# The copies of rotated q and k on GpSimd's DMA queue alone, in a two-layer hybrid trunk

## The chip, the cores and the metric

One core of a Trainium2 chip. Its engines are PE (TensorE, matmuls), DVE (VectorE), ACT (ScalarE), POOL (GpSimd) and SP (SyncE, which computes nothing and issues transfers). The metric is the device time of one execution in microseconds, as the median of the runs.

## The reference

Two layers over 256 positions of width 1024. Each layer normalises x, projects it by one wide matrix and feeds three mixers, whose outputs are gated, summed, projected and added to x; a squared-ReLU MLP follows. The part that matters here is the attention mixer: 24 heads of width 64 in three groups of eight, with rotary q and k. Rotation pairs the first and second half of a head:

```python
t1, t2 = jnp.split(tf, 2, axis=-1)
return jnp.concatenate([t1 * cos - t2 * sin, t2 * cos + t1 * sin], axis=-1)
...
for g, (window, dilation) in enumerate(DILATED_GROUPS):
    o, lse = dilated_group_attention(qf[:, :, g], kf[:, :, g], vf[:, :, g], window, dilation)
...
o = jnp.sum(wts * o, axis=0).reshape(B, S, ATTN_OUT_WIDTH)
```

The other two mixers are a gated linear recurrence (conv of 4 taps, scan) and a convolution of 31 taps with a layer norm.

## The kernel before

All weights stream through the core as chunks of 1 MB (128 partitions x 2048 floats), 92 in each layer. `weights` (L508) loads a chunk into one of two buffers `raw` through SP's queue, then ACT casts it to the high part `whi` and DVE subtracts that to give the low part `wlo`; a matmul is then done in three products (high by high, high by low, low by high). A `raw` buffer is free again when DVE has made both halves of `wlo`.

Inside a layer the chunks come in the order of the list `ORDER` (L38): v, the recurrence's inputs, the convolution's inputs, then blocks of q and k mixed with gates (`ga`, `gb`, `gc`) and outputs (`oa`, `ob`, `oc`) of the mixers. After that come the output projection, and the MLP's `up` and `dn`.

`rope` (L932) handles one block of q or k: four heads of one group. The matmul leaves the two halves of the heads apart: the first halves of the four heads in column block 0, the second halves in block 1, 32 partitions to a head. DVE makes `r1` from PSUM in three instructions (two products and a sum). For the scores each head needs its 64 rows together, so eight DMA copies of 32 partitions x 256 floats (32 KB) put `r1` into buffers `qk`, one for each head pair `hp` and group `g`. For each of the four heads, the first half goes through POOL's queue and the second through SP's queue (L951). There are twelve blocks in a layer, so 192 copies in all, 96 on each queue. A head pair's scores need six blocks' worth: 24 copies, twelve on each queue.

`scores` (L958) does 12 matmuls for a head pair and a half of the positions into the one PSUM buffer `sc`; DVE then adds the mask and takes the maximum (`sm`, `mx`, L972), ACT the exponential, and PE transposes the result (`tp`).

The order of the instructions on every engine is written out ahead by a planner (`Sched.run`, L252). It simulates the engines with a price for each operation, always takes the ready one with the longest way to the end, and emits the engines' orders. A DMA has two prices: what it occupies its issuing engine (`DMA_ISSUE`, L103: 600 ns on SP and ACT, 1040 ns on POOL) and, on one simulated transfer device, its bytes at 360 per ns with 500 ns ahead of them and 900 ns behind. `WHERE` (L44) names main matmuls before which the eight score groups must have been placed. On the chip each engine works through its list in order and waits for what is not there yet; what stands behind a waiting instruction in its list waits too. POOL's list also holds small memsets (`xp`, `upad`), the loads of the recurrence's gate weights (`lwr`) and gains, and a few tiny arithmetic operations of the norms.

Of the kernel before, what the change touches and what calls it, by code (L numbers as in the profile page):

```python
# [14 lines left out]
T = 256  # L15
# [84 lines left out]
           ("DVE", "PE"): 256, ("PE", "PE"): 2, ("ACT", "ACT"): 143, ("DVE", "DVE"): 127}  # L100
DMA_RATE = 0.36
MARGIN = 15000
DMA_ISSUE, DMA_START, DMA_DONE = {"SP": 600, "POOL": 1040, "ACT": 600}, 500, 900  # L103
LINE = 128
PSUM_TAGS = ("mm", "tp", "sc")
UNPADDED = PSUM_TAGS + ("st",)
# [270 lines left out]
def trunk_kernel(ctx: ExitStack, tc: tile.TileContext, x_d, pos_d, w_d, lruw_d, par_d, gain_d, const_d, id_d, out_d):  # L377
    nc = tc.nc
# [9 lines left out]
    def slot(name, dt=F32, shape=(P, 2, T)):  # L388
        return S.buf(sp, shape, dt, "s2", name, NSLOT)

    def mm_ps(name, shape=(P, 2, T), ring=True):
        return S.buf(pp, shape, F32, "mm", name, 4, ring)
# [13 lines left out]
    def views(*xs):  # L406
        return [x for x in xs if isinstance(x, View)]
# [19 lines left out]
    def tt(out, a, b, op):  # L427
        return S.op("DVE", 1.042 * out.n + 68,
                    lambda: nc.vector.tensor_tensor(out=out.ap(), in0=a.ap(), in1=b.ap(), op=op), [a, b], [out])  # L429
# [18 lines left out]
    def dma(eng, out, in_, nbytes):  # L448
        def fn():
            o = out.ap() if isinstance(out, View) else out  # L450
            i = in_.ap() if isinstance(in_, View) else in_
            eng.dma_start(out=o, in_=i)

        e = {id(nc.gpsimd): "POOL", id(nc.scalar): "ACT"}.get(id(eng), "SP")
        o = S.op(e, DMA_ISSUE[e], fn, views(in_), views(out))
        o.dma = nbytes / DMA_RATE / 1e3
        return o
# [50 lines left out]
    def weights(l, name, spread=False):  # L508
        c = CIDX[name]
        assert c == used[l], (name, c, used[l])  # L510
        used[l] += 1
        nm = f"{name}_{l}"
        raw = S.buf(wp, (P, CHUNK), F32, "raw", f"raw_{nm}", NRAW)
        if l or c:
            o = dma(nc.sync, raw.all(), w_d[l * NCH + c], CHUNK * P * 4)
            if l == 0 and c in late:
                S.follow(o, late[c])
        else:
            for s in range(2):
                o = dma(nc.sync, raw[:, s * HALF:(s + 1) * HALF], w_d[0][:, s * HALF:(s + 1) * HALF], HALF * P * 4)  # L520
                if ORDER[0][0] == "v":
                    S.follow(o, x1_load)
        if spread:
            hs, ls = [], []
            for q in range(4):
                hs.append(slot(f"whi_{nm}{q}", F32R, (P, 512)))
                ls.append(slot(f"wlo_{nm}{q}", F32R, (P, 512)))
                for o in split(hs[q].all(), ls[q].all(), raw[:, q * 512:(q + 1) * 512]):
                    o.prep = True
            return [(Quarters(hs[2 * s:2 * s + 2]), Quarters(ls[2 * s:2 * s + 2])) for s in range(2)]  # L530
        offs = (3 * LINE // 8, LINE // 8) if KIND[name] != "as" else (3 * LINE // 8,) * 2 if name[:2] in ("v1", "v2") else (0, 0)
        hi = Shifted(S.buf(wp, (P, CHUNK + LINE // 2), F32R, "whi", f"whi_{nm}", NHI), offs[0])
        lo = Shifted(S.buf(wp, (P, CHUNK + LINE // 2), F32R, "wlo", f"wlo_{nm}", NHI), offs[1])
        n = HALF if l == 0 and c < 2 else PREP
        for b in range(0, CHUNK, n):
            for o in split(hi[:, b:b + n], lo[:, b:b + n], raw[:, b:b + n]):
                o.prep = True
        return [(Part(hi, s * HALF), Part(lo, s * HALF)) for s in range(2)]
# [204 lines left out]
    for l in range(L):  # L743
# [12 lines left out]
        def gemm(name, w, ps, rhs):  # L756
            n0 = len(S.ops)
            ws_mm(ps, w, rhs)
            starts[name] = S.ops[n0]
# [172 lines left out]
        def rope(nm, g, j):  # L932
            w = weights(l, f"{nm}{g}{j}")
            ps = mm_ps(f"{nm}{g}{j}_{l}")
            gemm(f"{nm}{g}{j}", w, ps, hr)
            t1 = slot(f"r1{nm}{g}{j}_{l}")
            t2 = slot(f"r2{nm}{g}{j}_{l}")
            tt(t1.all(), ps.all(), cosT.all().map(lambda a: a[:, None, :].to_broadcast([P, 2, T])), OP.mult)
            tt(t2.all(), ps.all().map(lambda a: a[:, ::-1, :]), sins.all(), OP.mult)
            tt(t1.all(), t1.all(), t2.all(), OP.add)  # L940
            qi = 0 if nm == "q" else 1
            for hh in range(4):
                hp = 2 * j + hh // 2
                if (hp, g) not in qk:
                    qk[hp, g] = slot(f"qk{hp}{g}_{l}")
                for ab in range(2):
                    p0 = (hh % 2) * 64 + ab * 32
                    d = qk[hp, g]
                    dv = View(d, ((p0, p0 + 32), (qi, qi + 1), (0, T)), T,
                              lambda t, p0=p0: t[p0:p0 + 32, qi, :])  # L950
                    dma(nc.sync if ab else nc.gpsimd, dv, t1[hh * 32:(hh + 1) * 32, ab, :], 32 * T * 4)  # L951

        PTt, pvps, oh, ol = {}, {}, {}, {}
        sm = {}
# [158 lines left out]
        for name in ORDER:  # L1113
            kind, a = name[:2], name[2:]
            if kind in ("oa", "oc", "ob") and kind not in seen:
                {"oa": attention, "oc": layer_norm, "ob": lru_scan}[kind]()
                seen.add(kind)
            if name[0] == "v":
                vproj(int(name[1]), name == ORDER[0])
            elif name[0] in "qk":  # L1120
                rope(name[0], int(name[1]), int(name[2]))
            elif kind in ("ga", "gb", "gc"):
                ths[kind, int(a)] = gate(kind, int(a))
            else:
                {"gl": lambda: glu(int(name[3])), "lx": lambda: lx(int(a)), "lg": lambda: lg(int(a)),
                 "lw": lambda: lru_gates(int(a)), "ob": lambda: lru_out(int(a)), "oa": lambda: attn_out(int(a)),
                 "oc": lambda: conv_out(int(a))}[kind]()
# [219 lines left out]
```

## Time and profile before

| | us |
|---|---|
| median of 3 runs | 1116.06 (1115.8 to 1116.9) |
| the profiled execution | 1113.95 |
| its span, first to last instruction | 1112.2 |
| PE busy | 1095.9 (99%) |
| DVE busy | 902.4 (81%) |
| ACT busy | 727.7 (65%) |
| POOL busy | 70.1 (6%) |

The granted clock of TensorE was 0.999 of full speed. SP's queue carried 200.05 MB, POOL's 8.40 MB. The copies from `r1q` and `r1k` landed 4.4 and 4.6 us after their issue on SP, 3.7 and 4.0 us on POOL (medians). Engine names in rows: PEld is the loading of weights into PE; a q behind an engine (SPq) is its sequencer. Where many instructions follow each other with no idle time, a row merges them and gives their count.

### The profile page before, as it was taken

Reading aid. Unit: us, or ns where it says so; the run is one execution under the profiler, and the core shown is the slowest. Engines: PE = TensorE matmul, PEld = TensorE weight load, DVE = VectorE, ACT = ScalarE, POOL = GpSimd, SP = SyncE. Lnnn points to the kernel's source line nnn. Section 1 sums busy time; section 2 is a strip of 40 time slices with the busy share of each in tenths; the row PEclk is TensorE's granted clock in tenths of the full one; section 3 lists DMA queues with packets and bytes.
Section 4 is the critical chain, followed back from the end, with each engine's and each line's share of the span. In section 5 each row is a group of like instructions: output and inputs, shape, how many; then the busy total and the mean of one; then the engine's idle time right before and its main releaser. Section 6 shows DMA issues by size and latency. Waiting matters only on the chain.

```text
span 1112.2 us, 20605 instructions
## 1 busy us (share of the span) xinstructions
PE 1095.9 (99%) x8258; PEld 1023.9 (92%) x8258; DVE 902.4 (81%) x1380; ACT 727.7 (65%) x1186; POOL 70.1 (6%) x156
## 2 busy tenths in 40 slices
PE   7999999999999999999999999999999999999997
PEld 6999999998899899989889999999988998998996
DVE  6999999999969865555679999999996889655554
ACT  5879948787775454444569896569676746444443
POOL 1000022111000110000000000221200001000000
PEclk9999999999999999999999999999999999999999
DMA  8664466554436565555555553764633364555551
GB/s 294 247 208 152 152 226 236 184 193 149 142 121 245 195 211 197 194 194 189 189 200 215 181 182 116 255 222 171 216 123 143 146 248 161 214 190 189 194 190 71
DMA packets 37650, 209.77 MB, mean 189 GB/s; under 512 B 6449, under 2 KB 9777, under 8 KB 14130
## 3 DMA queue, kind: packets, MB, share of 16 engines
q1 hardware_dynamic: 32976, 200.05, 50.9%
q0 software_dynamic: 4576, 8.40, 2.3%
q8 instruction: 65, 1.06, 0.4%
q14 instruction: 31, 0.25, 0.1%
q10 hardware_dynamic: 2, 0.00, 0.0%
HBM read 201.08 MB, written 1.05 MB: 182 GB/s over the span
## 4 chain that ended last, share of the span: by engine, by line
PE 82%; DVE 10%; ACT 4%; DMA 2%; issue 1%; SPq 0%; DVEq 0%; ACTq 0%
PE dn L476 15%; PE up L476 14%; PE glu L476 8%; PE v L476 6%; PE ga L476 4%; PE gc L476 4%; PE wo L476 4%; PE oc L476 4%; PE lx L476 3%; PE k L476 3%; PE q L476 3%; PE lg L476 2%; PE ob L476 2%; PE ua L476 2%; PE oa L476 2%; PE pv L476 1%
## 5 line engine op out<-in xcount | busy, mean ns | idle before, releaser
L429 DVE TENSOR_TENSOR wlo_dn<-raw_dn,whi_dn 128x1024 fp32r<-128x1024 f32 (+1 forms) x66 | 76.7, 1190 | 71.2 <-ACT whi_dn L416 71.2
L416 ACT CAST whi_dn<-raw_dn 128x1024 fp32r<-128x1024 f32 (+1 forms) x66 | 65.4, 1023 | 78.9 <-PE dn L476 41.0
L433 DVE SCALAR_TENSOR_TENSOR c<-upad,parh,c 128x256 f32<-128x256 f32 x256 | 110.6, 477 | 0.1
L476 PE MATMUL up<-hl_mlp,whi_up 128*128 128x256 f32 x448 | 107.9, 277 | 0.0
L476 PE MATMUL up<-hh_mlp,whi_up 128*128 128x256 f32 x448 | 107.9, 277 | 0.0
L429 DVE TENSOR_TENSOR wlo_up<-raw_up,whi_up 128x1024 fp32r<-128x1024 f32 x56 | 67.3, 1222 | 48.2 <-ACT whi_up L416 48.2
L476 PE MATMUL dn<-whi_dn,uh 128*128 128x512 f32 x256 | 99.8, 390 | 0.0
L476 PE MATMUL dn<-wlo_dn,uh 128*128 128x512 f32 x256 | 99.8, 390 | 0.0
L423 ACT ACTIVATE cpd<-upad,parh 128x256 f32<-128x256 f32 x224 | 95.3, 499 | 5.7 <-DVE c L429 5.1
L416 ACT CAST whi_up<-raw_up 128x1024 fp32r<-128x1024 f32 x56 | 57.1, 1047 | 51.7 <-PE dn L476 25.4
L476 PEld LDWEIGHTS up<-hh_mlp,whi_up 128*128 128x128 f32 x448 | 84.1, 188 | 0.5
L476 PEld LDWEIGHTS up<-hl_mlp,whi_up 128*128 128x128 f32 x448 | 84.1, 188 | 0.5
L476 PE MATMUL dn<-whi_dn,ul 128*128 128x512 f32 x256 | 70.0, 389 | 0.0
L476 PE MATMUL up<-hh_mlp,wlo_up 128*128 128x256 f32 x448 | 69.4, 277 | 0.0
L429 DVE TENSOR_TENSOR cpd<-cpd 128x1024 f32<-128x1024 f32 (+2 forms) x84 | 63.0, 773 | 0.3 <-ACT cpd L423 0.3
L476 PE MATMUL glu<-hh_mix,whi_glu 128*128 128x256 f32 x256 | 61.2, 276 | 0.0
L476 PE MATMUL glu<-hl_mix,whi_glu 128*128 128x256 f32 x256 | 61.2, 276 | 0.0
L476 PEld LDWEIGHTS up<-hh_mlp,wlo_up 128*128 128x128 f32 x448 | 59.4, 188 | 0.0
L476 PEld LDWEIGHTS dn<-whi_dn,ul 128*128 128x128 f32 x256 | 48.1, 188 | 10.0
L476 PEld LDWEIGHTS dn<-wlo_dn,uh 128*128 128x128 f32 x256 | 48.1, 188 | 9.6
L476 PEld LDWEIGHTS dn<-whi_dn,uh 128*128 128x128 f32 x256 | 48.1, 188 | 9.5
L476 PEld LDWEIGHTS glu<-hl_mix,whi_glu 128*128 128x128 f32 x256 | 48.1, 188 | 0.0
(309 smaller groups left out, 3446.6 us busy)
## 6 DMA issues: line engine op xcount, KB each, us to landing
raw_dn<-w_in_stream SPq DMA_DIRECT2D x32, 1024.0 KB, 4.8
raw_up<-w_in_stream SPq DMA_DIRECT2D x28, 1024.0 KB, 4.8
raw_glu<-w_in_stream SPq DMA_DIRECT2D x16, 1024.0 KB, 4.9
raw_q<-w_in_stream SPq DMA_DIRECT2D x12, 1024.0 KB, 5.0
raw_k<-w_in_stream SPq DMA_DIRECT2D x12, 1024.0 KB, 4.8
raw_v<-w_in_stream SPq DMA_DIRECT2D x11, 1024.0 KB, 4.9
raw_lx<-w_in_stream SPq DMA_DIRECT2D x8, 1024.0 KB, 4.8
raw_lg<-w_in_stream SPq DMA_DIRECT2D x8, 1024.0 KB, 4.8
```

The source lines that it names most:

```text
L416: nc.scalar.copy(out.ap(), in_.ap())
L423: nc.scalar.activation(out.ap(), in_.ap(), func, scale=val(scale), **kw)
L429: lambda: nc.vector.tensor_tensor(out=out.ap(), in0=a.ap(), in1=b.ap(), op=op), [a, b], [out])
L433: lambda: nc.vector.scalar_tensor_tensor(out=out.ap(), in0=a.ap(), scalar=val(s), in1=b.ap(), op0=op0, op1=op1), [a, b] + views(s), [out])
L476: nc.tensor.matmul(out.ap(), lhsT=lhs.ap(), rhs=rhs.ap(), start=start, stop=stop)
```

## The change

All eight copies of a block go through POOL's queue, and the planner's price of a DMA on POOL is that of the other queues.

```diff
@@ -100,7 +100,7 @@
-DMA_ISSUE, DMA_START, DMA_DONE = {"SP": 600, "POOL": 1040, "ACT": 600}, 500, 900
+DMA_ISSUE, DMA_START, DMA_DONE = {"SP": 600, "POOL": 600, "ACT": 600}, 500, 900
@@ -948,7 +948,7 @@
                     dv = View(d, ((p0, p0 + 32), (qi, qi + 1), (0, T)), T,
                               lambda t, p0=p0: t[p0:p0 + 32, qi, :])
-                    dma(nc.sync if ab else nc.gpsimd, dv, t1[hh * 32:(hh + 1) * 32, ab, :], 32 * T * 4)
+                    dma(nc.gpsimd, dv, t1[hh * 32:(hh + 1) * 32, ab, :], 32 * T * 4)
```

The price enters the planner for every DMA that POOL issues, not for the copies alone, and the planner then writes the order of all engines anew.

## Rows read from the trace of the kernel before

**Rows 1.** The page, part 1: busy us, share of the span, count.
```profile
PE 1095.9 (99%) x8258; PEld 1023.9 (92%) x8258; DVE 902.4 (81%) x1380; ACT 727.7 (65%) x1186; POOL 70.1 (6%) x156
```
**Rows 2.** Timeline of PE: start us, us, instruction, count [idle before <-releaser].
```profile
169.76 1.18 PE L476 MATMUL sc<-qk 64*128 64x256 f32 x12
174.78 1.18 PE L476 MATMUL sc<-qk 64*128 64x256 f32 x12 [0.82 <-DVE mx L972]
...
193.04 1.18 PE L476 MATMUL sc<-qk 64*128 64x256 f32 x12
...
265.49 1.18 PE L476 MATMUL sc<-qk 64*128 64x256 f32 x12
...
716.60 1.18 PE L476 MATMUL sc<-qk 64*128 64x256 f32 x12
723.61 1.18 PE L476 MATMUL sc<-qk 64*128 64x256 f32 x12 [1.40 <-DVE mx L972]
...
760.92 0.66 PE L483 MATMUL tp<-ident,sm 128*128 128x128 f32 x4 [0.55 <-ACT sm L423]
...
813.57 1.18 PE L476 MATMUL sc<-qk 64*128 64x256 f32 x12
```
**Rows 3.** Windows: us, busy of PE, PEld, DVE, ACT, POOL (count), PEclk, DMA share, GB/s.
```profile
152.00:170.00 18.00, 18.00 (x160) 17.87 (x160) 17.38 (x21) 7.28 (x9) 5.91 (x12) 1.00 0.82 278
700.00:719.00 19.00, 19.00 (x171) 18.72 (x170) 18.21 (x25) 7.43 (x9) 5.91 (x12) 1.00 0.79 267
```
**Rows 4.** Chain of waits ahead of the stall at 174.78: start us, us, what.
```profile
160.64 0.68 DVE r1k L429
161.32 2.29 DVE wlo_gb L429 x2
...
164.44 5.44 DMA raw_ob<-w_in_stream
...
172.19 1.22 DVE wlo_ob L429
```
**Rows 5.** Copies on SP about 163.5: count, ns min/median/max, first and last start; landing.
```profile
L452 SPq DMA_DIRECT2D qk<-r1k x2: 522/556/589, 163.2 to 163.7; - x2
...
DMA to landing us min/median/max: 4.4/4.6/4.8
```
**Rows 6.** Chain of waits ahead of the stall at 723.61.
```profile
702.59 6.23 DMA raw_gb<-w_in_stream
...
710.00 2.37 DVE wlo_gb L429 x2
...
712.39 6.32 DMA raw_ob<-w_in_stream
```
**Rows 7.** All copies into qk: issue ns min/median/max on SP and POOL.
```profile
L452 SPq DMA_DIRECT2D qk<-r1q x48: 507/578/1402, 152.3 to 808.1; - x48
L452 POOL DMA_DIRECT2D qk<-r1q x48: 496/496/517, 152.8 to 807.0; - x48
```
**Rows 8.** The last copy on SP ahead of the scores at 193.04.
```profile
L452 SPq DMA_DIRECT2D qk<-r1k x1: 1513/1513/1513, 186.7 to 186.7; - x1
...
DMA to landing us min/median/max: 4.8/4.8/4.8
```
**Rows 9.** The last copies on SP ahead of the scores at 265.49.
```profile
L452 SPq DMA_DIRECT2D qk<-r1q x2: 507/544/581, 258.9 to 259.5; - x2
...
DMA to landing us min/median/max: 6.3/6.5/6.7
```
**Rows 10.** The last copy on SP ahead of the scores at 716.60.
```profile
L452 SPq DMA_DIRECT2D qk<-r1k x1: 588/588/588, 711.2 to 711.2; - x1
...
DMA to landing us min/median/max: 5.5/5.5/5.5
```
**Rows 11.** The last copies on SP ahead of the scores at 813.57.
```profile
L452 SPq DMA_DIRECT2D qk<-r1q x2: 582/992/1402, 806.6 to 808.1; - x2
...
DMA to landing us min/median/max: 4.4/5.1/5.7
```

## The prediction

> **What bounds the kernel now.** I read the page's busy shares first: the reader is to see PE busy for 1095.9 of 1112.2 us, DVE for 81% [rows 1]. A busy PE still hides stalls, so I then read PE's timeline for idle time ahead of an instruction. In the two stretches in which the rotated q and k are made and used there are three such places: 0.82 us and 1.40 us ahead of a score group, and 0.55 us ahead of a transposition of the softmax [rows 2]. That is 2.77 us together, and it is all that this change can win back from PE as its order now stands; PE's other work is of fixed size. The windows of the two copy bursts come next: PE busy without a break (18.00 of 18.00 and 19.00 of 19.00 us), DVE at 97% and 96%, the DMA engines at 0.82 and 0.79, POOL busy 5.91 us with 12 copies each time [rows 3]. So beside PE, DVE and the DMA engines are both nearly full there, and neither gets less work by the change.
>
> **What is moved.** Each q or k block issues eight copies of 32 KB, four by SP and four by POOL; 96 of the 192 in the program go from SP to POOL. SP's sequencer gets them off its hands, POOL issues them instead, the 16 DMA engines carry the same bytes. The planner's price of a DMA on POOL goes from 1040 to 600 ns, so the planner writes another order for every engine from the first POOL transfer on (the eight loads of the gates' weights and the gains are re-priced with the copies).
>
> **What SP gives back.** The chain of waits is followed back from the two stalls at score groups. In layer 0 the stalled scores waited for the maximum on DVE, which stood in DVE's order behind the low half of a weight block (wlo_ob), which waited for raw_ob. The buffer of raw_ob came free when wlo_gb ended at 161.32 + 2.29 = 163.61; SP issued the load at 164.44, since copies of k were in front of it, the last from 163.7 on [rows 4, 5]. So here SP's queue did hold a weight load, by 0.83 us, and that is as long as the stall (0.82). In layer 1 the same chain shows the opposite: raw_ob went out at 712.39, when wlo_gb ended at 710.00 + 2.37 = 712.37 [rows 6]. The copies were not in its way. What is slow there is the transfer: 6.23 and 6.32 us for a megabyte, against 5.44 in layer 0 [rows 4, 6], with the DMA engines 79% busy; copies from another queue take the same room. I take 0.8 us as won, with bounds of 0 (DVE, at 97%, has the maximum late anyway) and 2.77 (all three stalls go).
>
> **What POOL takes on.** A copy on POOL lasts 496 ns (496 to 517), on SP 507 or more, 578 in the median [rows 7]. A batch of 24 copies feeds a head pair's scores. Twelve on each queue cost POOL 12 x 0.496 = 5.95 us; all 24 cost 11.9 us. In the window of 18 us POOL was idle for 12 us [rows 3], so most of the extra 5.95 us finds room; but the end of a batch is bunched. The last k product of the first batch ends at 160.64 + 0.68 = 161.32 [rows 4], with eight copies still to go: on POOL alone the eighth would start at 161.32 + 7 x 0.496 = 164.8, against 163.7 before [rows 5], 1.1 us later; the whole 5.95 us if the room found is none. I take 2.5 us, nearer to the lower end because of the 12 idle us.
>
> Whether a later landing costs anything is read from how close the scores stand behind it. A landing is the last issue plus its time to land. Layer 0: 163.7 + 4.4 = 168.1, scores at 169.76, room 1.6 us; 186.7 + 4.8 = 191.5, scores at 193.04, room 1.5; 259.5 + 6.3 = 265.8, scores at 265.49, room none (-0.3) [rows 2, 5, 8, 9]. Layer 1: 711.2 + 5.5 = 716.7, scores at 716.60, room -0.1; 808.1 + 4.4 = 812.5, scores at 813.57, room 1.1 [rows 2, 10, 11]. A delay at the first group of a layer is also absorbed by the stall ahead of its second group (0.82 and 1.40), which DVE ends at the same time anyway.
>
> The planner knows of the longer queue: by its prices a batch took POOL 12 x 1.04 = 12.5 us and now 24 x 0.6 = 14.4, so it expects the inputs up to 1.9 us later and puts weight matmuls of other stages ahead of the scores. Bounds of that shift are 0 and 1.9; I take 1.5, since the last eight copies, issued back to back, are where its price counts in full. Then 2.5 - 1.5 = 1.0 us of lateness is left at each group, and only the group without room pays: 1.0 + 0.3 = 1.3 us at 265.49. The four others have 1.1 us or more, stalls counted.
>
> Here the Trainium skill speaks against the change: DMA: Bandwidth & Descriptors, section "Issuing engines are not separate DMA queues", says that transfers of all issuing engines run on the same 16 DMA engines and that another issuer saves only the issue time. The trace agrees for the layer-1 chain above, where a free SP queue still got a 6.32 us load [rows 6]; by the rule alone the 0.83 us at 164.44 would be the whole gain.
>
> **Sum.** -0.8 + 1.3 = +0.5 us. On the profiled execution's own 1113.95 us (span 1112.2) that is 1114.45; the median of the runs shown is 1116.06, 2.11 above it, so the forecast in medians is 1116.6. About 0.2%, 2.2 us, is what a measurement of this kernel can tell from no change.
>
> **Rivals.**
> *No change that can be measured* (forecast, 1116.6; own range 1114.2 to 1118.2). For it: PE has only 2.77 us to give, and both bounds of the shift leave gates with room. Chance 0.52.
>
> *The weight stream runs free.* Loads start as soon as a buffer is released, DVE gets its split work earlier, and the three stalls go: 1116.06 - 2.77 = 1113.3. For it: the 0.83 us at 164.44. Against it: in layer 1 the load was not held by copies, and the third stall is a softmax on ACT, not a weight. Chance 0.15.
>
> *The copies come late to the scores.* One mechanism, at the five score groups above: PE reaches the group in its written order, the last copies are still in POOL's queue, and every matmul behind waits. With no shift by the planner the prices are 2.5 less room: 2.5 - 1.6 - 0.8 = 0.1; 2.5 - 1.5 = 1.0; 2.5 + 0.3 = 2.8; 2.5 + 0.1 - 1.4 = 1.2; 2.5 - 1.1 = 1.4; sum 6.5, less 0.8 won, gives +5.7, 1121.8. With a shift of 0.9 they are 0, 0.1, 1.9, 0.3 and 0.5, +2.0 with the gain, 1118.1; it decides from there on. In the middle it gives 1120.0. For it: two groups start within 0.3 us of the landing. Against it: the planner prices POOL at 600 where the trace shows 496, so it errs to the late side. Chance 0.30.
>
> *POOL cannot issue at this pace.* If a copy on POOL had to sit out the DVE instruction beside it, some 1.2 us like half of wlo_gb (2.29 for two) [rows 4], a batch would take 24 x 1.2 = 29 us instead of 11.9, 17 us late, less 2.4 and 1.3 us of room at the first group of the two layers: about 30 us, 1146. Against it: no copy on POOL took over 517 ns while DVE was 97% busy [rows 3, 7]. Chance 0.03. The Trainium skill, SBUF — State Buffer, section "SBUF: two separate sides", has such a rule: descriptors of POOL's DMAs cannot be written while DVE holds the shared port in a two-port mode. The trace shows no such hold.
>
> **How the numbers follow.** Faster by over 0.2% is the free weight stream, 0.15. Slower is the two last, 0.33. The rest, 0.52, is no change. The range reaches down past 1113.3 to 1112.9 and up to 1120.8, which takes in most of the late copies; left out are their upper end, POOL's pace and a little below, some 0.17.
>
> **What would show it.** Right: POOL's copies still near 496 ns, twice as many; no copies among SP's issues; raw_ob of layer 0 issued at once when its buffer is free, and the 0.82 us stall smaller; the 6 us transfers of layer 1 as long as before; idle time of PE ahead of scores within 2 us of the 2.22 us now. Wrong: PE idle 1 us or more ahead of several score groups (late copies); the three stalls gone (free stream); a copy on POOL of 1 us (pace); or new stalls of PE at places that no copy feeds, which would mean that the planner's new order, and not a queue, sets the result.

## The result and the profile after

| | before | after |
|---|---|---|
| median of the runs timed together | 1116.48 us (1115.80 to 1119.24) | 1126.06 us (1124.98 to 1126.51) |
| ratio to before, 95% interval | | 1.0074 (1.0055 to 1.0092) |
| profiled execution | 1113.95 us, span 1112.2 | 1126.46 us, span 1124.4 |

The change makes the kernel slower by 0.74%, outside the range. The page, as in [rows 1]:

```profile
PE 1102.0 (98%) x8258; PEld 1028.9 (92%) x8258; DVE 902.4 (80%) x1380; ACT 728.9 (65%) x1186; POOL 117.6 (10%) x252
```

PE has the same 8258 matmuls, yet is busy 6.1 us longer (1102.0 against 1095.9) and idle 6.1 us longer (22.4 against 16.3): that is the whole 12.2 us of span. Two things have to be explained, idle time and slower matmuls. PE's timeline, answering to [rows 2], shows the first:

```profile
173.55 0.89 PE L476 MATMUL sc<-qk 64*128 64x128 f32 x4 [0.35 <-DMA qk<-r1k]
...
178.18 1.06 PE L476 MATMUL sc<-qk 64*128 64x256 f32 x10 [0.71 <-DVE mx L972]
...
720.43 0.94 PE L476 MATMUL sc<-qk 64*128 64x256 f32 x8
726.24 1.17 PE L476 MATMUL sc<-qk 64*128 64x128 f32 x4 [4.87 <-DMA qk<-r1k]
...
728.35 0.41 PE L476 MATMUL gb<-hh_mix,whi_gb 128*128 128x256 f32 x1
...
756.50 0.82 PE L476 MATMUL sc<-qk 64*128 64x128 f32 x4 [1.54 <-DMA qk<-r1k]
...
760.20 0.65 PE L483 MATMUL tp<-ident,sm 128*128 128x128 f32 x4 [1.32 <-ACT sm L423]
```

A score group of 12 now breaks after eight products and waits for the last copies of k: 4.87 us at the first group of layer 1, 1.54 us at a later one. The five waits come to 8.79 us, against 2.77 us in [rows 2]; that is the idle time. The windows (columns as in [rows 3]) show the second; the first of them answers to [rows 3], and even at a granted clock of 1.00 it has 152 matmuls in 17.95 us where before has 160 in 18.00:

```profile
152.00:170.00 18.00, 17.95 (x152) 17.75 (x152) 16.87 (x21) 8.49 (x9) 10.02 (x21) 1.00 0.72 233
...
720.00:725.00 5.00, 1.37 (x13) 1.02 (x11) 4.70 (x8) 4.32 (x9) 1.96 (x4) 0.98 0.62 233
725.00:730.00 5.00, 3.76 (x16) 3.57 (x17) 2.50 (x7) 1.08 (x4) 0.00 (x0) 0.50 0.60 225
730.00:735.00 5.00, 5.00 (x40) 4.71 (x38) 3.58 (x7) 4.57 (x10) 1.73 (x4) 0.84 0.04 8
```

After the 4.87 us the granted clock is 0.50, the 1.2 GHz level, and a matmul of 128x256 that takes 0.28 us at 2.4 GHz takes 0.41. From 727.34 us, where PE has started again, to 731.6, where the clock is back, the same matmuls fall another 2.0 us behind those of before (8.1 to 10.1). POOL's timeline of the batch that was late (start, us, count, idle time before and who ended it):

```profile
703.38 1.99 POOL L452 DMA_DIRECT2D qk<-r1q  x4 [83.21 <-DVE r1q L429]
707.33 0.99 POOL L452 DMA_DIRECT2D qk<-r1k  x2 [1.96 <-DVE r1k L429]
708.90 2.94 POOL L452 DMA_DIRECT2D qk<-r1k  x6 [0.59 <-ACT whi_gb L416]
712.40 1.97 POOL L452 DMA_DIRECT2D qk<-r1q  x4 [0.55 <-DMA qk<-r1k]
716.37 1.97 POOL L452 DMA_DIRECT2D qk<-r1q  x4 [2.00 <-DVE mg L433]
721.04 1.96 POOL L452 DMA_DIRECT2D qk<-r1k  x4 [2.71 <-issue]
```

The last of the 24 copies goes out at 722.5 us, 11.3 us later than in [rows 10]. The 11.8 us of issuing are as forecast; the gaps are not: 0.55 us for the landing of an earlier copy of its own queue, 2.00 us for a merge on DVE (`mg`) that frees the buffer `qk`, and 2.71 us in which POOL waits for nothing that the profile shows. All copies of the program, and then the last four of this batch with their landing:

```profile
L452 POOL DMA_DIRECT2D qk<-r1q x96: 498/498/517, 155.2 to 824.2; - x96
L452 POOL DMA_DIRECT2D qk<-r1k x96: 496/498/498, 159.1 to 819.7; - x96
...
L452 POOL DMA_DIRECT2D qk<-r1k x4: 496/498/498, 721.0 to 722.5; - x4
...
DMA to landing us min/median/max: 4.0/4.5/4.9
```

On SP the change does what it says. In layer 0 DVE ends `wlo_gb` at 164.62 + 2.36 = 166.98 and the load goes out 0.03 us later, where it stood 0.83 us behind copies [rows 4]:

```profile
164.62 2.36 DVE L429 TENSOR_TENSOR wlo_gb<-raw_gb,whi_gb 128x1024 fp32r<-128x1024 f32 x2 [0.99 <-ACT whi_gb L416]
```
```profile
167.01 0.33 SPq L452 DMA_DIRECT2D raw_ob<-w_in_stream  x1
```

### The profile page after: what moved, and what is told of

Its sections match the earlier page's. It is cut to its first block, busy times and chain, and to the rows that moved or that the text cites. A ratio compares the mean times of both kernels' runs of the same rounds, so it can differ in the third digit from the quotient of the medians.

```text
span 1124.4 us, 20504 instructions
## 1 busy us (share of the span) xinstructions
PE 1102.0 (98%) x8258; PEld 1028.9 (92%) x8258; DVE 902.4 (80%) x1380; ACT 728.9 (65%) x1186; POOL 117.6 (10%) x252
## 5 line engine op out<-in xcount | busy, mean ns | idle before, releaser
L452 POOL DMA_DIRECT2D qk<-r1q x96 | 47.2, 499 | 198.4 <-DVE r1q L429 145.6
```

## The experiments

Theory Q: one queue brings the last copies of a batch later than two did, and PE waits. Theory P: the new price of 600 ns makes the planner put the scores too early, whoever issues the copies. All ratios are to the kernel before on the same chip, with their 95% interval.

**The price alone, copies split as before.**

```diff
-DMA_ISSUE ... {"SP": 600, "POOL": 1040, "ACT": 600}
+DMA_ISSUE ... {"SP": 600, "POOL": 600, "ACT": 600}
```

> The planner's price of a DMA on POOL is 600 as in the changed kernel, the copies stay split over SP and POOL. Queue theory (one queue lands 24 copies too late): no loss without the move, 1114 to 1119 us, PE idle ahead of the score groups near the 2.2 us of before. Plan theory (the new price makes a plan whose scores come too early): most of the loss is here, 1122 us or more.

1124.35 us, ratio 1.0072 (1.0048 to 1.0095): as slow as the whole change, with no copy moved. PE's timeline:

```profile
170.86 0.85 PE L476 MATMUL sc<-qk 64*128 64x128 f32 x4 [3.23 <-DMA qk<-r1k]
...
724.96 1.32 PE L476 MATMUL sc<-qk 64*128 64x128 f32 x4 [2.77 <-DMA qk<-r1k]
```

So P holds by itself: with a cheaper POOL the scores stand ahead of the landing of k in both layers. The first scores of layer 1 follow 5438 matmuls, those of before 5462.

**All copies on POOL in the order of before** (the odd ones are planned as SP's, by a new argument `plan` of the helper `dma`).

```diff
-  dma(nc.sync if ab else nc.gpsimd, dv, t1[...], 32 * T * 4)
+  dma(nc.gpsimd, dv, t1[...], 32 * T * 4, plan=nc.sync if ab else nc.gpsimd)
```

> The planner plans the old kernel, odd copies as SP's at its price; only the instruction is issued by POOL, at the place of the old plan. Queue theory: the score groups stand where they stood and the last copies land 2 to 6 us later, so PE idles ahead of them and the time is 1121 to 1130 us. Plan theory: 1115 to 1118 us.

1127.97 us, ratio 1.0096 (1.0067 to 1.0124). PE's timeline, then POOL's:

```profile
724.18 0.99 PE L476 MATMUL sc<-qk 64*128 64x128 f32 x4 [5.47 <-DMA qk<-r1k]
...
762.19 1.12 PE L483 MATMUL tp<-ident,sm 128*128 128x128 f32 x4 [3.70 <-ACT sm L423]
```
```profile
165.72 0.50 POOL L452 DMA_DIRECT2D qk<-r1k  x1 [1.34 <-DMA qk<-r1q]
...
715.44 0.50 POOL L452 DMA_DIRECT2D qk<-r1k  x1 [1.85 <-DMA qk<-r1q]
718.81 0.99 POOL L452 DMA_DIRECT2D qk<-r1q  x2 [2.87 <-issue]
```

Q holds too, in layer 1 alone. In layer 0 the last copy goes out at 167.7, 4.0 us later than in [rows 5], and no score waits, since nothing but a wait of 1.34 us for copies in flight is in the way. In layer 1 it goes out at 720.3, 9.1 us later than in [rows 10]: the same wait is 1.85 us and a gap of 2.87 us without a cause follows. That gap stands ahead of POOL's 129th DMA in every kernel that issues so many: 2.71 us after the change, 2.87 here. The kernels with split copies issue 110 on POOL and so have no 129th.

**The order of after, odd copies on SP.**

```diff
-  dma(nc.gpsimd, dv, t1[...], 32 * T * 4)
+  dma(nc.sync if ab else nc.gpsimd, dv, t1[...], 32 * T * 4, plan=nc.gpsimd)
```

> The planner plans the changed kernel, all copies as POOL's at 600; but the odd ones are issued by SP at the place of the new plan. Queue theory: two queues land the batch earlier, the 4.9 us idle of PE in layer 1 falls below 1.5 us and the time is 1115 to 1119 us. Plan theory: the order of the engines is that of the changed kernel and its loss stays, 1123 to 1127 us.

1121.34 us, ratio 1.0032 (1.0013 to 1.0051), between the two forecasts. PE's timeline, then POOL's:

```profile
174.92 0.84 PE L476 MATMUL sc<-qk 64*128 64x128 f32 x4 [2.37 <-DMA qk<-r1k]
...
203.87 0.70 PE L476 MATMUL sc<-qk 64*128 64x128 f32 x4 [0.93 <-DMA qk<-r1k]
...
726.17 0.70 PE L476 MATMUL sc<-qk 64*128 64x128 f32 x4 [1.87 <-DMA qk<-r1k]
...
755.40 0.73 PE L476 MATMUL sc<-qk 64*128 64x128 f32 x4 [1.34 <-DMA qk<-r1k]
```
```profile
719.13 0.99 POOL L452 DMA_DIRECT2D qk<-r1q  x2 [4.85 <-DVE mg L433]
```

The order alone costs about 0.3%; the queue alone, in the experiment before, about 1%; together they cost 0.74%, so the two do not add up. Yet PE's waits for copies come to 6.5 us here, against 6.8 in the kernel after: two queues do not bring the copies of this order in time. The first batch of each layer shows what is the order's and what the queue's (us, layer 0 / layer 1):

| | last k product ends | last copy goes out | between |
|---|---|---|---|
| before | 161.3 / 709.4 | 163.7 / 711.2 | 2.4 / 1.8 |
| price alone, copies split | 162.7 / 716.7 | 165.2 / 718.6 | 2.5 / 1.9 |
| order of before, all on POOL | 161.3 / 710.5 | 167.7 / 720.3 | 6.4 / 9.7 |
| order of after, copies split | 163.7 / 714.8 | 169.1 / 721.2 | 5.4 / 6.4 |
| after | 163.6 / 711.8 | 171.3 / 722.5 | 7.7 / 10.7 |

With the price alone the copies follow their products as before, and only the scores are early. In the order of after, the merge ahead of the copies makes them 3.0 and 4.6 us later on two queues already; the one queue adds 2.3 and 4.3 us, and 2.71 of the 4.3 are the gap ahead of the 129th DMA.

**All copies on POOL at a price of 800.** `"POOL": 600` becomes 800 in the kernel after.

> The changed kernel with a price of 800 instead of 600 for POOL, so that the planner expects a batch of 24 copies to take 19.2 us and not 14.4 and puts the scores later. Queue theory: the copies land as late, but the scores wait less; 1117 to 1123 us, with the idle time ahead of the first score group of layer 1 under 2 us. Plan theory by the price alone (nearer to the old price is better): about 1119 us or less as well; it differs in that the copies then land no later than with the split.

1132.06 us, ratio 1.0128 (1.0093 to 1.0164), the slowest of all, and outside both forecasts. No score waits for a copy any more; PE waits for DVE instead:

```profile
185.71 1.18 PE L476 MATMUL sc<-qk 64*128 64x256 f32 x12 [1.88 <-DVE mx L972]
...
200.14 0.36 PE L476 MATMUL q<-hh_mix,whi_q 128*128 128x256 f32 x1 [4.17 <-DVE r2q L429]
```

A price is no cure: at 800 ns the planner takes a batch for 24 x 0.8 = 19.2 us of POOL and puts 5534 matmuls ahead of the first scores of layer 1, 72 more than before has.

**Layer 0 split, layer 1 on POOL, order of before.** Layer 1 then starts at POOL's 61st DMA, and the 129th comes late in it. (The numbers 85 to 132 in the expectation were miscounted: the first batch is 61 to 84.)

```diff
+  dma(nc.sync if ab and l == 0 else nc.gpsimd, dv, t1[...], 32 * T * 4, plan=nc.sync if ab else nc.gpsimd)
```

> Order of the kernel before; in layer 0 the copies are split over SP and POOL as before, in layer 1 all are issued by POOL. The first batch of layer 1 is then POOL's DMAs 85 to 108, the second 109 to 132 (with layer 0 on POOL as well they were 109 to 132 and 133 to 156). Theory A, queue and pause: the last k copies of layer 1's first batch are late by the pace of one queue with eight copies in flight alone, without the pause of 2.87 us ahead of POOL's 129th DMA, so TensorE's idle ahead of the first scores of layer 1 falls from 5.47 us to about 2.6 (2 to 3.5) and the time is 1120 to 1124; the pause comes back at the 21st copy of the second batch. Theory B, one queue alone: the pause is hidden behind the waits on copies in flight, the idle stays over 4.5 us, 1125 to 1129. Theory C, the pause belongs to the first batch of layer 1 and not to the count: a gap over 2 us that the profile puts down to issue stands in the first batch again, and the idle stays over 4.5 us.

1121.36 us, ratio 1.0039 (1.0014 to 1.0064); the twelve runs go from 1117.13 to 1129.55, and the profiled one took 1124.80. PE's timeline, then POOL's:

```profile
720.32 1.08 PE L476 MATMUL sc<-qk 64*128 64x128 f32 x4 [2.23 <-DMA qk<-r1k]
...
759.94 1.11 PE L483 MATMUL tp<-ident,sm 128*128 128x128 f32 x4 [4.21 <-ACT sm L423]
```
```profile
712.35 0.50 POOL L452 DMA_DIRECT2D qk<-r1k  x1
715.46 0.50 POOL L452 DMA_DIRECT2D qk<-r1k  x1 [2.61 <-DMA qk<-r1q]
...
794.96 1.97 POOL L452 DMA_DIRECT2D qk<-r1k  x4 [2.71 <-issue]
```

As theory A had it: the first batch has no pause, the idle time falls from 5.47 to 2.23 us, and the pause of 2.71 us comes at 794.96, which is again the 129th DMA on POOL. It belongs to the count, not to the place. What is left in the first batch is the wait of 2.61 us. Its cause can be read from this kernel's rows: the weight load on SP, and the landing of the nine copies issued at 708.4 to 712.3:

```profile
708.72 0.33 SPq L452 DMA_DIRECT2D raw_q<-w_in_stream  x1
```
```profile
DMA to landing us min/median/max: 6.0/6.0/6.0
...
DMA to landing us min/median/max: 1.7/6.1/6.4
```

`raw_q` takes 6.0 us, to 714.7. The copy issued just ahead of it, at 708.4, lands in 1.7 us; those behind it take up to 6.4 us and land when the load has landed. POOL's DMAs count on eight semaphores in turn (111 to 118 in the trace), so that each waits for the landing of the one eight before it: in no run does one go out ahead of that landing, and every such wait ends 0.28 us behind it. Eight copies, from 708.9 to 712.35, fill the eight places; the ninth can't go before the first of them has landed, at 715.2. Split over two queues a batch has sixteen places, and no copy on POOL waits so in any run with split copies. The Trainium skill, DMA: Bandwidth & Descriptors, section "Issuing engines are not separate DMA queues", says that transfers of all issuers share the same DMA engines; the trace agrees, with copies of one queue that take up to 6.4 us behind a load of another.

**The kernel after, with four DMAs fewer on POOL ahead of layer 1,** so that the 129th is the first copy of the second batch.

```diff
-  dma(nc.gpsimd, raw.all(), lruw_d[4 * l + j], 512 * P * 4)
+  dma(nc.sync if l == 0 else nc.gpsimd, raw.all(), lruw_d[4 * l + j], 512 * P * 4, plan=nc.gpsimd)
```

> The kernel after in the same order, but the four loads of the gates' weights of layer 0 are issued by SP, so that POOL has four DMAs fewer ahead of layer 1 and its 129th is the first copy of layer 1's second batch, behind an idle of POOL of some 10 us. Theory, the pause ahead of the 129th DMA is part of the loss: the last four k copies of the first batch go out about 2.7 us earlier, TensorE's idle ahead of the first scores of layer 1 falls from 4.87 us to 1.8 to 2.8, and the time from 1126.1 to 1120 to 1123.5; a gap put down to issue of 2.7 us stands at the first copy of the second batch or is hidden in POOL's idle. Rival, the pause only fills a wait that would be there anyway (the copy eight before, the weight load in flight): idle over 4 us, 1125 to 1127.

1123.32 us, ratio 1.0052 (1.0036 to 1.0068). PE's timeline, then POOL's:

```profile
718.89 0.47 PE L476 MATMUL sc<-qk 64*128 64x128 f32 x2 [0.88 <-DMA qk<-r1k]
...
721.59 0.47 PE L476 MATMUL sc<-qk 64*128 64x128 f32 x2 [2.22 <-DMA qk<-r1k]
...
726.52 1.18 PE L476 MATMUL sc<-qk 64*128 64x256 f32 x12
```
```profile
714.80 1.96 POOL L452 DMA_DIRECT2D qk<-r1k  x4 [0.69 <-DMA qk<-r1q]
730.47 1.96 POOL L452 DMA_DIRECT2D qk<-r1q  x4 [13.70 <-issue]
```

SP's load of that time, the landing of the four copies from 714.80 on, and a window that answers to [rows 3]:

```profile
716.12 0.33 SPq L452 DMA_DIRECT2D raw_gb<-w_in_stream  x1
```
```profile
DMA to landing us min/median/max: 3.2/3.6/5.2
...
152.00:170.00 18.00, 18.00 (x161) 18.00 (x160) 17.81 (x21) 8.16 (x9) 11.96 (x24) 1.00 0.80 279
```

The wait falls from 4.87 to 3.10 us in two parts (1.8 to 2.8 were expected). The pause has moved to the second batch, whose first copy waits for a score group: it starts at 730.47, 2.8 us after that group ends (726.52 + 1.18 = 727.70), where the kernel after has it within 0.2 us of the group's end. The two parts have the load between them: three of the four copies go out ahead of it, the last at 716.26, 0.14 us behind it, and that one takes 5.2 us and holds PE for the 2.22. So the pause is part of the wait; the time lies inside 1120 to 1123.5, but its interval overlaps that of the kernel after, and the profiled execution is the fastest of the six (1120.66), so the size of the pause's share stays loose.

**The kernel after, with the planner told that copies land later,** by 2.0, 3.0 and 1.0 us. All copies stay on POOL at 600 ns, pause included.

```diff
-  dma(nc.gpsimd, dv, t1[...], 32 * T * 4)
+  dma(nc.gpsimd, dv, t1[...], 32 * T * 4).late = 2000
...
-  return p.dma + DMA_START + DMA_DONE if p.dma else ...
+  return p.dma + DMA_START + DMA_DONE + p.late if p.dma else ...
```

> The kernel after, but the planner is told that each copy lands 2.0 us later than it takes it to (all copies still on POOL at a price of 600). Theory, the scores are planned ahead of their copies: the waits of TensorE for k copies (4.87 and 1.54 us in layer 1) shrink to under 1.5 us together, the granted clock stays at 1.00 between 725 and 735 us, and the time falls to 1117 to 1122. Rival, one queue can't carry the batch in any order (the copies are late for what follows the scores too): the wait only moves to the softmax and the transposes, and the time stays at 1124 to 1128.

> The kernel after with a later landing of 3.0 us in the plan instead of 2.0. Theory, the plan is the cause: no wait of TensorE for a copy is left (under 0.5 us together) and the time is 1115 to 1119. Rival, scores that start later leave VectorE without work: TensorE waits for the softmax, 1119 to 1124.

> The kernel after with a later landing of 1.0 us in the plan, between none (a ratio of 1.0074) and 2.0 us (1.0010). Theory, the loss follows how far the scores are planned ahead of their k copies: the waits for k copies in layer 1 (6.41 us in the kernel after, 1.66 with 2.0 us) come to 2 to 4.5 us together and the time is 1119 to 1123. Rival, the order is what it is by chance and the size of the allowance says nothing: outside of that, 1123 to 1128, or 1116 and less, with waits that do not lie between.

| later by | ratio | PE's waits for k in layer 1 |
|---|---|---|
| 0 (kernel after) | 1.0074 (1.0055 to 1.0092) | 4.87 + 1.54 us |
| 1.0 us | 1.0000 (0.9983 to 1.0016), 1117.55 us | 2.63 us |
| 2.0 us | 1.0010 (0.9990 to 1.0030), 1118.16 us | 1.66 us |
| 3.0 us | 1.0037 (1.0020 to 1.0055), 1122.36 us | 1.23 us |

PE's timeline with 1.0 us, then POOL's:

```profile
723.59 0.81 PE L476 MATMUL sc<-qk 64*128 64x128 f32 x4 [2.63 <-DMA qk<-r1k]
```
```profile
719.24 1.97 POOL L452 DMA_DIRECT2D qk<-r1k  x4 [3.53 <-issue]
```

The waits shrink as the allowance grows, and with 1.0 or 2.0 us the loss is gone, although POOL's queue and its pause are what they were (the last copy still goes out 10.6 and 10.4 us after the last k product): the queue alone does not set the time. The first two microseconds put 12 more weight matmuls each ahead of the first scores of layer 1, the third 4. The steps of the time were not as expected: 1.0 us gave all back where half was expected, and with 2.0 us the waits came to 1.66 us, not under 1.5, and the clock fell to 0.66 between 725 and 730 us, where 1.00 was expected. With 3.0 us the rival shows: PE waits 3.35 us for a maximum on DVE in layer 0.

**The same allowance of 2.0 us, and the pause moved** as above, by the same two edits.

> The kernel after with the later landing of 2.0 us in the plan and the same four loads issued by SP: the idle of 1.66 us ahead of the first scores of layer 1 vanishes (under 0.5), the granted clock between 725 and 730 us is 1.00 and not 0.66, and the time is 1114 to 1117 against 1118.2 with the pause. Rival, VectorE's queue sets the end there: no change, 1117 to 1119.

1119.72 us, ratio 1.0031 (1.0017 to 1.0046): no gain against 1.0010, where 1114 to 1117 us were expected; the two intervals overlap, so no loss is shown either. The profiled execution took 1124.03 us, 4.3 above the median. PE's timeline, then the windows behind the two waits:

```profile
182.78 2.08 PE L476 MATMUL sc<-qk 64*128 64x256 f32 x12 [2.80 <-DVE mx L972]
...
734.74 1.49 PE L476 MATMUL sc<-qk 64*128 64x256 f32 x12 [2.34 <-DVE mx L972]
```
```profile
185.00:190.00 5.00, 5.00 (x27) 5.00 (x28) 4.43 (x10) 4.26 (x8) 3.35 (x8) 0.57 0.42 149
...
735.00:740.00 5.00, 5.00 (x34) 4.78 (x33) 5.00 (x8) 3.89 (x9) 1.31 (x3) 0.66 0.49 200
```

The first scores of layer 1 no longer wait for copies, as expected, but the second group waits for DVE, and the clock falls in both places. That is the rival's place, DVE's queue behind the copies, though its 1117 to 1119 us are passed too; how far a median run has these two waits is not shown.

**The kernel before with the allowance of 1.0 and 2.0 us**, copies split.

> The kernel before (copies split over SP and POOL, POOL priced at 1040), but the planner is told that each copy lands 1.0 us later. Theory: before has no wait on a copy that counts, so a later landing in the plan takes nothing away; the order shifts by a few matmuls, as it does with every other price, and the time is 1116 to 1121. Rival, before's scores already stand too near their copies: 1112 to 1115.

> As the run with 1.0 us, with 2.0 us. Theory: 1116 to 1123, since scores that start later leave VectorE idle ahead of them (97% busy in this stage). Rival, a freer order: 1112 to 1115.

1116.67 us, ratio 0.9993 (0.9978 to 1.0009), and 1116.90 us, 0.9991 (0.9976 to 1.0007): no change. The kernel before has nothing to gain from it, and no version tried here beats it.

## Why the prediction was wrong

The step that failed is "What POOL takes on": "I take 2.5 us", with bounds of 1.1 and 5.95 us, and the 1.5 us set against it, which left 1.0 us of lateness. The last issue came 11.3 us later in layer 1 (722.5 against 711.2) and 7.6 us later in layer 0 (171.3 against 163.7). Of that, 2.5 and 2.3 us stand already in the products, which come later in the kernel after; counted from the last k product the lateness is about 8.8 and 5.3 us. The queue's own part, 4.3 and 2.3 us in the new order and 7.9 and 4.0 in the old, was 2.5 us in the sum; the new order's part, 4.6 and 3.0 us, was nothing there. I sized the step by POOL's issuing time and its idle share in a window [rows 3]. What the runs showed in its place is three waits that no view of the kernel before contains. A copy waits for the one eight before it: 1.34, 1.85 and 2.61 us in the order of before, but only 0.55 us here, and behind that it waits for the merge in any case. A copy waits for the merge that frees its buffer (2.00 us here, 4.85 on two queues), which the new order put ahead of it. And there is the pause ahead of the 129th DMA (2.71 us).

The one cost in the sum, 1.3 us at 265.49, did not come: that group starts at 268.08 in the kernel after and waits for nothing. The 4.87 us stand at the first group of layer 1, which the sum let go free for the stall behind it, and the 1.54 us at the third, which the prediction does not list.

The pause also has a second price. It pushes the last four copies to 721.04, behind the weight load that SP issues at 720.50, and they land 4.0 to 4.9 us after their issue; with four DMAs fewer on POOL three of the four go out ahead of that load and land within 3.8.

"The planner knows of the longer queue" was right in size, 1.5 us taken: 12 more matmuls stand ahead of the scores of layer 1. It was wrong in what it meant. The same new order holds the copies back by 3.0 and 4.6 us, and the shift is no allowance for landings at all: the planner takes a copy to land some 1.4 us and its transfer after the issue, and the trace shows 4.0 to 4.9. At 1040 ns the price seems to have made up for that, though it was meant for the issue alone. The price by itself (ratio 1.0072) and the allowance of 1.0 us (1.0000) fit this from both sides.

The sum had no term for the clock. A wait of 4.87 us was followed by a granted clock of 0.50, and the matmuls lost another 2.0 us. Of the 12.2 us of span, half is idle time and half slower or longer matmuls. Some 2.8 us of it lie in layer 0, where no wait exceeds 0.71 us. There the 696 weight matmuls of 128x256 between 140 and 243 us take 1.9 us more than before: in the window of 152 to 170 us they follow each other every 0.118 us, not every 0.113 as in [rows 3], both at a granted clock of 1.00. The same order with four DMAs fewer has 161 of them in 18.00 us there and ran layer 0 about 3 us faster, in one profiled execution each; so the order alone does not explain it, and the cause stays open.

Right were POOL's pace (496 to 517 ns, so the fourth rival falls), SP without copies, and `raw_ob` issued at once. The stall behind it went from 0.82 to 0.71 us; the 0.8 us that I booked as won were not. Of the two long transfers of layer 1, `raw_gb` stayed long (6.23 and then 6.87 us), `raw_ob` did not (6.32 and then 5.08). The rival "copies come late to the scores" had the mechanism and, of the two groups without room, one as the place. Its upper end of 1121.8 us was too low for the same reason as the forecast: it too was built on 2.5 us, with nothing for the new order's own delay or for the clock.

## What to carry to other kernels

Count how many transfers a queue can have in flight before two queues are merged into one, and how long a large load holds them back: in the order of before these two, and not the issuing time alone, made the last of a burst late. Then look at what a new order puts ahead of the transfers: here a merge that frees their buffer held them on one queue and on two. A price in a planner may be standing in for something else, here the landing time; change it only together with what it covers, or give that a term of its own. A wait of PE can be dearer than its length: behind one of 4.87 us the matmuls lost another 2.0 us at the lower clock.

## What the runs showed of the hardware that was not expected

Ahead of the 129th DMA on POOL's queue there is a pause: 2.71, 2.87 and 2.76 us (kernel after, order of before, price 800), and 2.71 us at another place where fewer went before; with the allowances it is 2.8 to 3.5 us. Why the pause is there was not found.

PE's wait and the clock behind it: 4.87 us gave 0.50 in the next window, 2.80 us gave 0.57, 2.34 us 0.66. A wait of 1.66 us was followed by 0.66 in one place and by 1.00 in another of the same kernel (2.0 us allowance, 724.52 and 180.57 us), and one of 2.37 us by 1.00 (order of after, copies split, 174.92 us). The shares between 0.50 and 1.00 are means over 5 us; in the traces the clock has these two levels alone. So the length of a wait does not tell the clock behind it.
